# Query-tile constants behind block 6 of a recurrence, and a full-precision sum in the last attention step alone

## The chip, the cores and the metric

One core of a Trainium2 chip. The metric is the device time in microseconds of one execution of the whole program, the median of three runs. Times inside the program come from one profiled execution. Its engines are TensorE (PE, with its weight loads PEld), VectorE (DVE), ScalarE (ACT), GpSimd (POOL) and SyncE (SP, which issues most DMAs); each takes its instructions in the order of its own queue.

## What is computed

One layer of a hybrid trunk on 2064 tokens (16 meta tokens and 2048 of the sequence) of width 1024, all in float32:

```python
p = rms_norm(h, norm_mix_pre) @ w_in
oa = rg_lru_group(...)                  # linear recurrence, 256 columns
ob = forgetting_attention_group(...)    # 8 heads of 64, causal, with a decay
oc = rwkv7_group(...)                   # matrix-state recurrence, 4 heads of 64
h = h + rms_norm(concat(oa, ob, oc) @ w_out, norm_mix_post)
f = causal_dwconv(rms_norm(h, norm_ffn_pre) @ ffn_up, ffn_conv)
h = h + rms_norm((gelu(gate) * val) @ ffn_down, norm_ffn_post)

# attention, per head
s = q @ k.T / 8 + (c[:, None] - c[None, :])      # c: running sum of log f
o = softmax(where(kpos <= qpos, s, -inf)) @ v
# rwkv7, per head and token
S = S * w_t - (S @ kk_t) (kk_t * a_t).T + v_t k_t.T ;  o_t = S @ r_t
```

## The kernel before, in words

Almost all of it keeps full precision by splitting an operand into a rounded part and a remainder and adding three fast products (`mm3`, lines 172 to 176, tiles `psp`, `pswo`, `psu`, `psd`).

The program has four parts. **First** the input projection in three parts of the sequence (lines 2125 and following; tile `psp`). Beside it, generators feed in the two recurrences: `recurrences` runs nine blocks (0 to 8, of 256 tokens, the last of 64). A block of the matrix recurrence has a front (`Rwkv.block`, and `chunks` up to `SOLVED`: scores `rwsc` at lines 1131 and 1136, transposes at 1160, a triangular solve of 15 steps that goes between POOL at 1178 and DVE at 1179) and an ending: small products that complete the inverse (1202 to 1254), **the sums** (lines 1269 to 1271: products `rps`, then `rwgt` and `rwrav` on DVE), **the states** (1281 to 1293: four products one after another, each with a copy to `rstate` at 1293; the fourth copy is the block's last state), and the output with its norm (1320 to 1359). The ending of one block comes after the front of the next, so at the end of the projection the ending of block 5 is under way and the fronts of 7 and 8 and the endings of 6, 7 and 8 are still to come. All these products go through two buffers `rps`, in the order of the program.

**Second** attention (`Attn`). There are 32 steps, of one head and 512 queries each: half 0 with the query blocks 0 and 1, half 1 with 2 and 3. A step has two passes. `maxima` makes rough products (`mx`, line 566) and takes each row's largest (line 571, `mc`), which goes into a row of the query tile `q2` (line 580). `weights` makes exact scores in two products (`sc`, 693 with `q1`, 694 with `q2`), their exp (698, tile `p`), the product with the values (716, `po`) and the sums of the weights (`acc`, 737, on POOL and DVE). The maxima run two steps ahead of the weights, so there are three buffers of each of the query tiles `q3` (for `mx`) and `q2`. Half of the rows of these tiles are constants, set on DVE at the very start of attention, when `Attn` is built: lines 469 and 487 to 489. Attention's first `mx` product needs those of its tiles.

At the end of a step, `ending` queues three pieces of work by a clock of score groups: the column sums of `acc` over partitions, their reciprocals, and the scaling. The sums come in two forms. `total` (767 to 776) splits `acc` on ACT and POOL and adds two fast products (772, 773). `single` (760 to 765) makes one full-precision product (762). The form is chosen by whether the queue for the step's small DMAs is POOL's:

```python
for d, f in zip(self.DELAYS, (single if queue is nc.gpsimd else total, invert, scale)):
```

`run` sets that queue when it comes to the last step. The `ending` of the step before is run inside the last step's `weights`, after its first group of scores, and so takes that queue and `single` too: two steps have it.

**Third** the output projection in 17 tiles (`pswo`), the first of which fill PE between the attention steps of half 1. Tiles 7 and 8 are held until the last but one step has ended; the eviction of tile 9 (line 168) is queued behind the last step's copy of its sums (line 763). **Fourth** the feed-forward layers (`psu`, `psd`).

What sets the order is a scheduler: for each engine it arranges the instructions by a timeline that it works out from their dependencies. `issue_after(x)` adds the rule that an instruction must stand behind `x` in the queue, if both are on the same engine.

Of the kernel before, what the change touches and what calls it, by code (L numbers as in the profile page):

```python
# [8 lines left out]
F32 = mybir.dt.float32  # L9
# [4 lines left out]
ALU = mybir.AluOpType  # L14
# [18 lines left out]
class Core:  # L33


    def __init__(self, tc, ctx):
        self.tc = tc
        self.nc = tc.nc
        self.ctx = ctx
        self.uid = 0  # L40
        nc = self.nc
        self.const = ctx.enter_context(tc.tile_pool(name="const", bufs=1))
        self.ident = self.const.tile([P, P], F32, name="ident")
        make_identity(nc, self.ident[:])
        self.flip = 0
        self.root = self.apart = False
        self.turns = 0

    def n(self, s):
        self.uid += 1  # L50
# [395 lines left out]
class Attn:  # L446
# [7 lines left out]
    def __init__(self, core, pool, psum, more, scr):  # L454
        self.core, self.pool, self.psum, self.more, self.scr = core, pool, psum, more, scr
        self.wide, self.bank, self.place, self.tail = False, 0, 0, False
        nc = self.nc = core.nc
        self.clock, self.later, self.serial, self.added = 0, [], 0, 0
        self.pending, self.loads, self.steps, self.beside = None, [], [], iter(())


        self.turn = {"k": 1, "k2": 1, "q2": 0, "q3": 0}
        self.ring = {s: [] for s in self.turn}
        for i in range(self.AHEAD + 1):
            q3 = pool.tile([P, 512], F32R, tag=f"q3_{i}", name=core.n("q3"), bufs=1)
            self.fixed(q3, None, self.ONES)
            self.ring["q3"].append(q3)
            q2 = pool.tile([P, 512], F32R, tag=f"q2_{i}", name=core.n("q2"), bufs=1)
            nc.vector.memset(q2[64:128].bitcast(F32), 0.0)
            self.ring["q2"].append(q2)  # L470
            if i > 1:
                continue
            k1 = pool.tile([P, 2, KHALF], F32R, tag=f"k1_{i}", name=core.n("k1"), bufs=1)
            self.rear(pool, f"k2_{i}")
            v1 = pool.tile([P, 2, NKT // 2 + 1, 64], F32, tag=f"v1_{i}", name=core.n("v1"), bufs=1)
            self.ring["k"].append((k1, v1))
# [16 lines left out]

    def next(self, s):
        self.turn[s] = (self.turn[s] + 1) % len(self.ring[s])
        return self.ring[s][self.turn[s]]

    def t(self, shape, tag, dt=F32, bufs=2):
# [162 lines left out]
    def weights(self, h, b, keys, queries, fill):  # L661
# [6 lines left out]
        nc, core, scr = self.nc, self.core, self.scr  # L668
        k1, k2, v1 = keys
        q1, q2, bias = queries  # L670
# [71 lines left out]
        def ending(po, acc):  # L742


            while len(self.later) > 8:
                self.later.pop(0)[2]()

            o, oh = self.t([64, 512], "o", bufs=4), self.t([64, 512], "oh")
            c1 = kt[1][2]
            nc.scalar.activation(oh[:, c1:n], po[64:128, c1:n], AF.Copy)  # L750
            if c1:
                nc.scalar.activation(o[:, :c1], po[0:64, :c1], AF.Copy)
            summed = nc.vector.tensor_tensor(o[:, c1:n], po[0:64, c1:n], oh[:, c1:n], op=ALU.add)
            if self.tail:
                self.reduced = summed
            g = n // 16
            dcol = self.t([16, 32], "dcol", bufs=4)
            rb, queue = [], self.queue

            def single():  # L760
                ps = self.mx()
                nc.tensor.matmul(ps[0:1, :n], core.ones_col[:].bitcast(F32), acc[:, :n], start=True, stop=True)
                core.acted = nc.scalar.activation(acc[0:1, :n], ps[0:1, :n], AF.Copy)
                queue.dma_start(scr["den"][h : h + 1, ts], acc[0:1, :n])
                queue.dma_start(dcol[:, :g], scr["den"][h, ts].rearrange("(p c) -> p c", c=g))

            def total():
                ah, al = (self.t([P, 512], "oh", F32R) for _ in range(2))
                core.acted = nc.scalar.activation(ah[:, :n], acc[:, :n], AF.Copy)
                nc.gpsimd.tensor_tensor(al[:, :n], acc[:, :n], ah[:, :n], op=ALU.subtract)  # L770
                ps = self.mx()
                nc.tensor.matmul(ps[0:1, :n], core.ones_col[:], ah[:, :n], start=True, stop=False)
                nc.tensor.matmul(ps[0:1, :n], core.ones_col[:], al[:, :n], start=False, stop=True)
                nc.scalar.activation(acc[0:1, :n], ps[0:1, :n], AF.Copy)
                queue.dma_start(scr["den"][h : h + 1, ts], acc[0:1, :n])
                queue.dma_start(dcol[:, :g], scr["den"][h, ts].rearrange("(p c) -> p c", c=g))

            def invert():
                rb.append(self.t([64, 512], "rb"))
                nc.vector.reciprocal(dcol[:, :g], dcol[:, :g])  # L780
                queue.dma_start(scr["rden"][h, ts].rearrange("(p c) -> p c", c=g), dcol[:, :g])
                queue.dma_start(rb[0][:, :n], scr["rden"][h : h + 1, ts].broadcast_to([64, n]))

            def scale():
                nc.vector.tensor_tensor(o[:, :n], o[:, :n], rb[0][:, :n], op=ALU.mult)
                queue.dma_start(scr["mix"][256 + 64 * h : 256 + 64 * h + 64, ts], o[:, :n])

            for d, f in zip(self.DELAYS, (single if queue is nc.gpsimd else total, invert, scale)):
                self.serial += 1
                self.later.append((self.clock + d, self.serial, f))  # L790
            self.later.sort(key=lambda x: x[:2])
# [31 lines left out]
    def run(self, pool, third):  # L823


        self.queue = self.nc.sync
        ready = []
        for half, bs in enumerate(((0, 1), (2, 3))):
            if half:
                self.rear(third, "k2_2")  # L830
                self.beside = self.meta(pool)
            for h in range(NH):
                self.wide = (half, h) >= WIDE
                keys = self.keys(h, 4 * bs[-1] + 5)
                for b in bs:
                    gen, total, out = self.maxima(h, b, keys), self.pieces(b), []

                    def fill(share, gen=gen, total=total, out=out):
                        while len(out) < min(total, share * total):
                            out.append(next(gen))  # L840

                    if len(ready) == self.AHEAD:
                        self.weights(*ready.pop(0), fill)
                    fill(1.0)
                    ready.append((h, b, keys, next(gen)))
        self.tail = True
        for i, step in enumerate(ready):
            if i == len(ready) - 1:
                self.queue = self.nc.gpsimd
            self.weights(*step, lambda share: None)  # L850
        self.flush()
        for _ in self.beside:
            pass
        while len(self.later) > 1:
            self.later.pop(0)[2]()
# [128 lines left out]
class Rwkv:  # L984
# [127 lines left out]
    def chunks(self, b, nch, sg, rav, bk, wc, bon):  # L1112
# [3 lines left out]
        nc, k, core = self.nc, self.k, self.core  # L1116
        tt = nc.vector.tensor_tensor
# [7 lines left out]
        for c0 in range(0, m2, 4):  # L1125
            m = min(4, m2 - c0)
# [8 lines left out]
            for h, ps in enumerate(pss):  # L1135
                tt(
                    sc[:, 2 * c0 + h : 2 * (c0 + m) : 2, 64:192], ps[:, :m], mask.to_broadcast([P, m, P]),
                    op=ALU.mult,
# [16 lines left out]
        for c in range(0, m2, 4):  # L1155
            m = min(4, m2 - c)
            for src, dst in ((bk, sc), (rav[:, :, 1:3], w3)):
                ps = self.ps().rearrange("p (c t) -> p c t", t=P)
# [48 lines left out]
        for i0, m in groups:  # L1207
            ps = self.ps().rearrange("p (i t) -> p i t", t=32)
# [54 lines left out]
        for c in range(0, m2, 4):  # L1263
            m = min(4, m2 - c)
            ps = self.ps().rearrange("p (c t) -> p c t", t=P)
            for i in range(m):
                for h in range(2):
                    j = 2 * (c + i) + h
                    nc.tensor.matmul(ps[64 * h : 64 * h + 64, i], ap[:, j], sc[0:64, j, 0:128], start=True, stop=True)
            tt(gt[:, c : c + m], ps[:, :m, 0:64], gt[:, c : c + m], op=ALU.add)  # L1270
            tt(rp[:, c : c + m], ps[:, :m, 64:128], rav[:, c : c + m, 0], op=ALU.add)


        st = k["st"]
# [10 lines left out]
        for c in range(nch):  # L1285
            for h in range(2):
                hs = slice(64 * h, 64 * h + 64)
                for p in range(2):
                    nc.tensor.matmul(
                        gain[hs, c, p], gt[hs, p * nch + c], st[hs, c, p], start=False, stop=True,  # L1290
                        skip_group_check=True,
                    )
            nc.vector.tensor_copy(st[:, c + 1], gain[:, c])
        yield

        ntl = -(-nch // 2)
# [1083 lines left out]
```

## Time and profile before

| | us |
|---|---|
| median of 3 runs | 2995.25 (2985.94 to 2998.46) |
| the profiled execution | 2995.96, of it the span 2994.3 |
| last input projection evicted | 878.9 |
| first and last `mx` product of attention | 890.5, 1487.3 |
| full-precision sums of the last two steps | 1508.5, 1540.6 |
| last output-projection product | 1645.2 |
| mean granted clock of TensorE | 0.976 |

The profile is read from the whole to the place: the page's busy shares say which engine has least idle time, the table by stage says where that engine idles and at what clock, and the timelines say what a single instruction waits for. Times are from the start of the span; a clock of 0.50 means that TensorE was granted half of its clock in that stretch.

### The profile page before, as it was taken

The numbers are of one execution on the slowest core, as the hardware profiler recorded it, in microseconds if no ns is written. First come the engines' busy times: TensorE is split into PE (matmuls) and PEld (weight loads), VectorE is DVE, ScalarE is ACT, GpSimd is POOL, SyncE is SP. The second block draws the span as 40 slices with busy tenths as digits, with TensorE's granted clock in tenths as the row PEclk, the third lists the DMA queues.
The fourth block names the chain that finished last, engine by engine and source line by source line (L and its number), as shares of the span: only waits on it lengthen the run. The fifth ranks groups of instructions, "written<-read, shape, count | busy, mean of one in ns | idle before, by whom it ended". The sixth has DMA issues, their size and how long they took to land.

```text
span 2994.3 us, 52802 instructions
## 1 busy us (share of the span) xinstructions
PE 2898.0 (97%) x18694; PEld 2486.3 (83%) x18694; DVE 2037.0 (68%) x3937; ACT 1480.8 (49%) x2858; POOL 1319.7 (44%) x1567
## 2 busy tenths in 40 slices
PE   6999999999999999999999999999999999999998
PEld 6998899888886655665568999999999999787887
DVE  5258644765677776565636998898778787656766
ACT  4246332443346554455634656666565665424333
POOL 1002122121223665666843667446655544656443
PEclk9999899999988999999999999999999999999999
DMA  6777469676644347544336565577777764436453
GB/s 210 239 235 226 135 230 310 203 242 194 199 129 101 95 109 208 134 113 109 77 96 212 183 198 179 173 220 211 208 208 218 222 198 128 158 116 220 145 174 120
DMA packets 469190, 530.49 MB, mean 177 GB/s; under 512 B 85710, under 2 KB 355736, under 8 KB 467372
## 3 DMA queue, kind: packets, MB, share of 16 engines
q1 hardware_dynamic: 468156, 526.17, 58.2%
q8 instruction: 147, 2.41, 0.3%
q0 software_dynamic: 768, 0.93, 0.1%
q14 instruction: 119, 0.97, 0.1%
HBM read 368.07 MB, written 158.90 MB: 176 GB/s over the span
## 4 chain that ended last, share of the span: by engine, by line
PE 59%; DVE 4%; POOL 2%; DMA 2%; ACT 2%; issue 2%; SPq 0%; DVEq 0%; POOLq 0%; ACTq 0%
PE psu L174 9%; PE psu L175 9%; PE psu L176 9%; PE po L716 4%; PE psd L174 4%; PE psd L175 4%; PE psd L176 4%; PE mx L566 2%; PE pswo L174 2%; PE pswo L176 2%; PE pswo L175 2%; PE sc L693 2%; PE sc L694 2%; POOL acc L737 1%; DVE mc L571 1%
## 5 line engine op out<-in xcount | busy, mean ns | idle before, releaser
L175 PE MATMUL psu<-xo,uw 128*128 128x344 f32 x1848 | 591.4, 320 | 0.0
L174 PE MATMUL psu<-xo,uw 128*128 128x344 f32 x1848 | 586.0, 322 | 2.7 <-ACT u L1828 1.2
L176 PE MATMUL psu<-xo,uw 128*128 128x344 f32 x1848 | 581.9, 320 | 1.3 <-POOL uw L1657 1.0
L174 PE MATMUL psp<-xh,wh 128*128 128x384 f32 (+2 forms) x1152 | 380.8, 331 | 0.0
L176 PE MATMUL psp<-xh,wl 128*128 128x384 f32 (+2 forms) x1152 | 378.0, 328 | 0.0
L175 PE MATMUL psp<-xl,wh 128*128 128x384 f32 (+2 forms) x1152 | 377.8, 328 | 0.0
L1657 DVE TENSOR_TENSOR uw<-uq,uw 128x512 fp32r<-128x512 f32 x341 | 320.3, 944 | 59.2 <-ACT uw L1656 56.7
L174 PEld LDWEIGHTS psu<-xo,uw 128*128 128x128 f32 x1848 | 345.8, 188 | 4.3 <-DVE vb L1848 1.8
L176 PEld LDWEIGHTS psu<-xo,uw 128*128 128x128 f32 x1848 | 345.7, 188 | 2.1 <-POOL uw L1657 1.3
L175 PEld LDWEIGHTS psu<-xo,uw 128*128 128x128 f32 x1848 | 347.1, 188 | 0.0
L1656 ACT ACTIVATE uw<-uq 128x512 fp32r<-128x512 f32 x462 | 287.9, 627 | 95.7 <-PE psu L176 44.4
L698 ACT ACTIVATE p<-sc,bias 128x512 f32<-128x512 f32 (+4 forms) x352 | 197.9, 590 | 142.3 <-PE sc L694 119.2
L571 DVE TENSOR_REDUCE mc<-mx 128x1 f32<-128x512 f32 (+6 forms) x352 | 190.0, 565 | 113.6 <-PE mx L566 80.1
L1796 DVE SCALAR_TENSOR_TENSOR uy<-psu,ffn_cols,uy 128x342 f32<-128x342 f32 (+1 forms) x390 | 220.4, 567 | 61.4 <-ACT uy L1794 59.7
L1804 POOL TENSOR_TENSOR uy<-uy,uy 128x342 f32<-128x342 f32 (+1 forms) x132 | 146.5, 1110 | 229.2 <-DVE uy L1796 55.9
L737 POOL TENSOR_TENSOR acc<-acc,p 128x512 f32<-128x512 f32 (+3 forms) x208 | 222.7, 1073 | 48.4 <-DVE acc L737 23.4
L1657 POOL TENSOR_TENSOR uw<-uq,uw 128x512 fp32r<-128x512 f32 x121 | 184.4, 1524 | 133.8 <-ACT uw L1656 116.0
L174 PEld LDWEIGHTS psp<-xh,wh 128*128 128x128 f32 x1152 | 220.1, 191 | 8.7 <-issue 7.3
L176 PEld LDWEIGHTS psp<-xh,wl 128*128 128x128 f32 x1152 | 220.1, 191 | 7.0 <-issue 5.1
L175 PEld LDWEIGHTS psp<-xl,wh 128*128 128x128 f32 x1152 | 220.1, 191 | 5.0 <-issue 3.2
L1657 DVE TENSOR_TENSOR fo<-u,fo 128x896 fp32r<-128x896 f32 x88 | 101.6, 1155 | 133.7 <-ACT fo L1656 133.2
L1656 ACT ACTIVATE fo<-u 128x896 fp32r<-128x896 f32 x88 | 81.2, 923 | 206.6 <-PE psd L176 118.1
(488 smaller groups left out, 6409.4 us busy)
## 6 DMA issues: line engine op xcount, KB each, us to landing
uq<-scr_us SPq DMA_DIRECT2D x220, 256.0 KB
uq<-in_ffn_up_dram SPq DMA_DIRECT2D x209, 256.0 KB
wl<-scr_wk SPq DMA_DIRECT2D x48, 512.0 KB
wh<-scr_wk SPq DMA_DIRECT2D x48, 512.0 KB
u<-scr_ff SPq DMA_DIRECT2D x88, 256.0 KB
scr_ff<-uy SPq DMA_DIRECT2D x110, 171.0 KB
raw<-in_w_in_dram SPq DMA_DIRECT2D x24, 512.0 KB
scr_wk<-wh SPq DMA_DIRECT2D x24, 512.0 KB
```

What stands on the lines that cost most here:

```text
L174: nc.tensor.matmul(out, ah, bh, start=first, stop=False, skip_group_check=more)
L175: nc.tensor.matmul(out, ah, bl, start=False, stop=False, skip_group_check=more)
L176: nc.tensor.matmul(out, al, bh, start=False, stop=last, skip_group_check=more)
L566: nc.tensor.matmul(ps[:rows, : e - a], q3[:, qo : qo + rows], k2[:, a:e], start=True, stop=not last)
L571: self.reduced = nc.vector.tensor_reduce(mc[:rows, i, ci : ci + 1], ps[:rows, : e - a], axis=AX.X, op=ALU.max)
L698: last = nc.scalar.activation(p[:rows, :w], ps[:rows, :w], AF.Exp, bias=bias[:rows, j : j + 1])
L716: mm = nc.tensor.matmul(po[at : at + 64, c0:n], v1[:rows, j], p[:rows, : n - c0], start=start and i < 2, stop=end and i + 2 >= len(group), ...
L737: eng.tensor_tensor(a, ps_[0][0][:rows, c0:n] if start and i == 1 else a, p[:rows, : n - c0], op=ALU.add)
L1656: core.nc.scalar.activation(hi, src, AF.Copy)
L1657: (eng or core.nc.vector).tensor_tensor(lo, src, hi, op=ALU.subtract)
L1796: core.conved = stt(y[:, :n], src[:, i : n + i], cw[:, 44 * i + cc : 44 * i + cc + 1], y[:, :n], op0=ALU.mult, op1=ALU.add)
L1804: core.pooled = nc.gpsimd.tensor_tensor(v[:, :n], g[:, :n], v[:, :n], op=ALU.mult)
```

## The change

Two things. The constants of the query tiles are no longer set when `Attn` is built: each buffer gets them when it is first taken (`next`), and the first buffer's stand behind the sums of the third block from the end, block 6 (`marks[-3]`, `summed`), the other two behind its last state (`moved`). And the sums of the weights are made by `single` only in the `ending` that is run after all steps, which is the last one's; the last but one goes back to `total`, still with POOL's queue for its small DMAs.

```diff
@@ Core.__init__
+        self.marks = []
@@ Attn.__init__
+        self.final = False
...
+        self.blank, self.begun = {s: [] for s in self.turn}, {s: 0 for s in self.turn}
         for i in range(self.AHEAD + 1):
             q3 = pool.tile([P, 512], F32R, tag=f"q3_{i}", name=core.n("q3"), bufs=1)
-            self.fixed(q3, None, self.ONES)
+            self.blank["q3"].append(lambda q3=q3: self.fixed(q3, None, self.ONES))
             self.ring["q3"].append(q3)
             q2 = pool.tile([P, 512], F32R, tag=f"q2_{i}", name=core.n("q2"), bufs=1)
-            nc.vector.memset(q2[64:128].bitcast(F32), 0.0)
+            self.blank["q2"].append(lambda q2=q2: nc.vector.memset(q2[64:128].bitcast(F32), 0.0))
@@ Attn.next
         self.turn[s] = (self.turn[s] + 1) % len(self.ring[s])
+        if self.blank[s] and self.begun[s] < len(self.ring[s]):
+            with self.core.tc.issue_after(self.core.marks[-3][min(self.begun[s], 1)].ins):
+                self.blank[s][self.turn[s]]()
+            self.begun[s] += 1
         return self.ring[s][self.turn[s]]
@@ Attn.weights, ending
-            for d, f in zip(self.DELAYS, (single if queue is nc.gpsimd else total, invert, scale)):
+            for d, f in zip(self.DELAYS, (single if self.final else total, invert, scale)):
@@ Attn.run
+        self.final = True
         self.flush()
@@ Rwkv.chunks
-            tt(rp[:, c : c + m], ps[:, :m, 64:128], rav[:, c : c + m, 0], op=ALU.add)
+            summed = tt(rp[:, c : c + m], ps[:, :m, 64:128], rav[:, c : c + m, 0], op=ALU.add)
...
-            nc.vector.tensor_copy(st[:, c + 1], gain[:, c])
+            moved = nc.vector.tensor_copy(st[:, c + 1], gain[:, c])
+        core.marks.append((summed, moved))
```

With the new code the numbers of later lines grow: 469 becomes 472, lines 487 to 492 become 490 to 495, those from 566 to 857 grow by 7, those from 858 to 1293 by 8, later ones by 9.

The order on DVE at the end of the input projection, before the change: `rwgt_9235` is the ending of block 5, `q_1446` and its neighbours are the query tiles.

```order
L1270 TENSOR_TENSOR rwgt_9235<-rps_9237,rwgt_9235 128x256
L1271 TENSOR_TENSOR rwrav_7292<-rps_9237,rwrav_7292 128x4x64
L487 MEMSET q_1446_11103 64x512
L469 MEMSET q_1447_11107 64x512
L487 MEMSET q_1451_11114 64x512
```

All constants stand between the two halves of block 5's sums and behind them, ahead of and among its states. With the change, DVE where the first constants are now (`rwgt_10203` is the ending of block 6, `rwxu_10567` belongs to block 7):

```order
L1278 TENSOR_TENSOR rwgt_10203<-rps_10216,rwgt_10203 128x256
L1279 TENSOR_TENSOR rwrav_8650<-rps_10216,rwrav_8650 128x4x64
L490 MEMSET q_1451_11110 64x512
L472 MEMSET q_1452_11111 64x512
L491 MEMSET q_1451_11110 3x512
L492 MEMSET q_1451_11110 1x512
L1201 STREAM_TRANSPOSE rwxu_10567<-rwxu_10567 64x512
L1301 COPY rstate<-rps_10228 128x128
```

The first buffer's constants moved back from row 1278 to row 1399 of DVE, past the front of block 7 and the ending of block 6; those of the other two stand 16 rows further on, behind the fourth copy of `rstate`.

PE before the change, just behind the last products of the input projection; `mx` and `sc` are attention's:

```order
L1281 MATMUL rps_9260<-rww_973_7341,rwsc_7340 64x64 x16
L1289 MATMUL rps_9260<-rstate,rwgt_9235 64x64 x4
L1320 MATMUL rps_9298<-rstate,rwrav_7292 64x64
L1289 MATMUL rps_9260<-rstate,rwgt_9235 64x64 x4
L1320 MATMUL rps_9298<-rstate,rwrav_7292 64x64
L566 MATMUL mx_11153<-k_1449_11110,q_1451_11114 128x144
```

And with the change, PE at its first `mx` product:

```order
L1277 MATMUL rps_10205<-rwsc_8670,rwxu_10174 64x128 x8
L1277 MATMUL rps_10216<-rwsc_8670,rwxu_10174 64x128 x8
L1115 MATMUL eps_10501<-rwsq_10443,bones 128x128
L1289 MATMUL rps_10228<-rww_1138_8671,rwsc_8670 64x64 x16
L1297 MATMUL rps_10228<-rstate,rwgt_10203 64x64 x4
L1329 MATMUL rps_10266<-rstate,rwrav_8650 64x64
L573 MATMUL mx_11145<-k_1449_11106,q_1451_11110 128x144
```

Attention's first `mx` product now stands behind the sums of block 6 instead of those of block 5. The 46 rows that it moved past are the rest of block 5's ending, the scores and transposes of block 7, block 6's ending up to its first state, small products of block 8, and two `sc` products of line 700 (693 before), which need no constants.

PE near the end of attention, before the change: `acc_16169` belongs to the last but one step, `sc` to the last.

```order
L694 MATMUL sc_16231<-q_1457_11129,k_1449_11110 128x512
L762 MATMUL mx_16266<-acc_16169,ones_col 1x512
L693 MATMUL sc_16236<-q_2832_15891,k_1453_11120 128x512
L694 MATMUL sc_16236<-q_1457_11129,k_1449_11110 128x512
L716 MATMUL po_16168<-p_16182,v_1455_11124 64x512
```

And with the change, the two products that take its place, among those of output tile 7 (`pswo`):

```order
L176 MATMUL pswo_17080<-wol,mh_17072 128x512
L779 MATMUL mx_16270<-oh_16266,ones_col 1x512
L177 MATMUL pswo_17080<-woh,ml_17073 128x512
L175 MATMUL pswo_17080<-woh,mh_17072 128x512
L176 MATMUL pswo_17080<-wol,mh_17072 128x512
L177 MATMUL pswo_17080<-woh,ml_17073 128x512
L175 MATMUL pswo_17105<-woh,mh_17072 128x512
L176 MATMUL pswo_17105<-wol,mh_17072 128x512
L177 MATMUL pswo_17105<-woh,ml_17073 128x512
L175 MATMUL pswo_17105<-woh,mh_17072 128x512
L780 MATMUL mx_16270<-oh_16267,ones_col 1x512
```

The sums of the last but one step stand some 30 rows later on PE, behind the products with the values and most of output tile 7's first half, and no score of the last step is behind them any more.

## The prediction

> **What bounds the kernel now.** First the page's busy shares and its chain of work that ended last.
>
> ```profile
> span 2994.3 us, 52802 instructions
> PE 2898.0 (97%) x18694; PEld 2486.3 (83%) x18694; DVE 2037.0 (68%) x3937; ACT 1480.8 (49%) x2858; POOL 1319.7 (44%) x1567
> PE 59%; DVE 4%; POOL 2%; DMA 2%; ACT 2%; issue 2%; SPq 0%; DVEq 0%; POOLq 0%; ACTq 0%
> ```
>
> TensorE (PE) is busy for 97% of the span and carries 59% of the chain, so an idle microsecond of PE is lost unless PE idles a microsecond less elsewhere. The change touches the stretch from the last input projection to the last attention step. Next view: busy time by stage (us of the stage; then busy us and instruction count of PE, PEld, DVE, ACT, POOL; then the granted PE clock, the DMA share and GB/s).
>
> ```profile
> 878.00:890.00 12.00, 10.84 (x90) 8.15 (x92) 8.47 (x22) 1.40 (x5) 8.06 (x6) 0.50 0.52 124
> 890.00:974.00 84.00, 77.34 (x693) 56.62 (x695) 64.05 (x188) 47.39 (x104) 28.44 (x53) 0.77 0.48 108
> 974.00:1122.00 148.00, 137.44 (x1207) 88.61 (x1201) 111.90 (x299) 86.49 (x184) 94.30 (x148) 0.94 0.43 103
> 1122.00:1200.00 78.00, 72.16 (x339) 39.59 (x339) 52.41 (x112) 38.26 (x70) 47.11 (x53) 0.93 0.73 207
> ```
>
> From 890 to 1122 PE is kept 92 to 93% busy because two things run side by side: the tail of the recurrence (blocks 5 to 8), a long chain of small products and DVE operations, and the first attention steps. The rows that fix the places:
>
> ```profile
> 878.88 0.42 DVE L241 SCALAR_TENSOR_TENSOR stl<-psp,sth 128x256 fp32r<-128x256 f32 x1 [0.66 <-ACT sth L240]
> 882.95 0.48 DVE L487 MEMSET q<- 64x512 f32 x1 [0.16 <-issue]
> 887.31 0.41 DVE L1271 TENSOR_TENSOR rwrav<-rps,rwrav 128x256 f32<-128x256 f32 x1
> L566 PE MATMUL mx<-k,q x352: 219/397/797, 890.5 to 1487.3; 128*128 128x512 f32 x72, 128*128 128x400 f32 x51, 128*128 128x128 f32 x16, 128*128 128x384 f32 x16
> 886.58 3.60 POOL L492 MEMSET k<- 1x2080 f32 x2
> L1271 DVE TENSOR_TENSOR rwrav<-rps,rwrav x2: 414/414/414, 970.9 to 973.2; 128x256 f32<-128x256 f32 x2
> ```
>
> The last projection is evicted at 878.9. The query constants are set from 882.95, the sums of block 5 end at 887.7, the first product of attention starts at 890.5, and the sums of block 6 end at 973.6.
>
> **The change, part by part: the constants.** By the order of the changed kernel the first constants stand behind the sums of block 6, and the first mx product behind them, with 46 rows of recurrence on PE that no attention product can pass (but for two sc products). The instructions are the same; what moves is all attention work that now lies between 890 and 974. So the sum is: the new start of attention, plus that work, less 974.
>
> *New start.* From the sums of block 5 (887.7) to those of block 6 (973.6) the chain takes 85.9 us with attention beside it. I cut it in four stages, at these ends:
>
> ```profile
> 917.01 0.42 DVE L1357 TENSOR_TENSOR rww<-rww,rps 128x256 f32<-128x256 f32 x1
> 925.77 0.69 DVE L1136 TENSOR_TENSOR rwsc<-rps,rmask 128x512 f32<-128x512 f32 x1 [0.23 <-PE rps L1131]
> 940.01 0.67 DVE L1212 TENSOR_TENSOR rwxu<-rps,rmask 64x512 f32<-64x512 f32 x1
> ```
>
> Whether PE runs at full or half clock there decides much, so clock rows first, four microseconds each: projections, then recurrence alone, then mostly attention.
>
> ```profile
> 872.00:876.00 4.00, 4.00 (x29) 3.19 (x28) 1.90 (x5) 1.04 (x4) 0.00 (x0) 1.00 0.20 68
> 880.00:884.00 4.00, 4.00 (x22) 2.17 (x20) 2.14 (x5) 1.02 (x4) 3.52 (x3) 0.50 0.86 218
> 884.00:888.00 4.00, 4.00 (x52) 3.55 (x54) 3.40 (x10) 0.00 (x0) 2.53 (x3) 0.50 0.42 98
> 916.00:920.00 4.00, 4.00 (x25) 2.42 (x23) 2.70 (x7) 2.77 (x7) 3.78 (x4) 1.00 0.77 176
> ```
>
> With the recurrence alone the clock stands at 0.50, though PE counts as busy for all 4 us. The Trainium skill (TensorE: Matmul & The Clock Gate, section on the HAM clock gate) says that the clock is full after about 3.4 us of sustained PE activity and half after an idle window of that length. Taken literally it would put the new stretch, in which PE has products most of the time, at full clock (the low ends below, about 9 us under the value taken); the trace does not agree, with 0.50 from 880 to 888 at 4.00 of 4.00 busy, and the measurement decides.
>
> The stages, now without attention:
>
> ```profile
> 887.70:917.40 29.70, 9.01 (x19) 0.55 0.86 184
> 918.15 1.16 PE L1131 MATMUL rps<-rwrav,rwbk 64*128 64x128 f32 x8
> 921.21 0.70 PE L1440 MATMUL eps<-rwlu,lru_ga_w 128*128 128x256 f32 x2
> 934.00 1.28 ACT L698 ACT_TABLE_LOAD   x1
> 940.70:973.60 32.90, 5.31 (x160) 4.96 (x160) 0.79 0.19 45
> 940.70:973.60 32.90, 3.93 (x32) 3.56 (x32) 0.79 0.19 45
> 940.70:973.60 32.90, 5.22 (x32) 4.09 (x32) 0.79 0.19 45
> 940.70:973.60 32.90, 2.18 (x32) 1.70 (x32) 0.79 0.19 45
> ```
>
> - Stage 1 (state, output of block 5; 29.7 us): attention's DVE reductions in it are 9.0 us (first row), the query constants some 2.5 more; the raw-row loads and the dependent small DVE operations stay. I let a little over half of that go: 23.2.
> - Stage 2 (scores of block 7; 9.1 us): four groups of 1.16 us and two gate pairs of about 1.2 us are 7.0 us at full clock, some 13 at half clock. So 7 to 13.
> - Stage 3 (transposes, first small products; 14.2 us): what goes is attention's exp and the table load it needs, about 3 us: 11.3.
> - Stage 4 (rest of block 6; 32.9 us): the last four rows are PE's time by line (L1202, L1244, L1254, L1269), 16.6 us at a mean clock of 0.79, so 13.2 at full clock; half clock makes at most twice that, and as part is latency I take 24. With about 5 us of evictions between them: 18 to 29.
>
> Together 59.5 to 76.5 us, so block 6's sums at 947 to 964; four memsets of 0.5 us follow, and attention starts at 949 to 966. I take **958**, the middle: rows show the half clock for recurrence alone, but parts of the chain are DVE's.
>
> *Work moved.* How much attention was done before 974, and what is it worth? Reductions (L571), then scores (L694), in three windows:
>
> ```profile
> 890.00:974.00 84.00, 18.34 (x38) 0.77 0.48 108
> 1122.00:1200.00 78.00, 35.96 (x65) 0.93 0.73 207
> 1400.00:1508.00 108.00, 39.76 (x70) 1.00 0.32 77
> 890.00:974.00 84.00, 10.15 (x27) 5.73 (x27) 0.77 0.48 108
> 1122.00:1200.00 78.00, 16.65 (x45) 8.65 (x45) 0.93 0.73 207
> 1400.00:1508.00 108.00, 32.77 (x91) 16.57 (x91) 1.00 0.32 77
> ```
>
> In the two windows without recurrence and without output projection attention does 110 pieces in 78 us and 161 in 108, 1.41 to 1.49 a microsecond. The 65 pieces before 974 are then worth 44 to 46 us; but they are the narrow ones (18.34/38 = 0.48 us a reduction against 0.55), so I take **39**. If some slip into PE's idle time of the two stages behind (148 - 137.4 and 78 - 72.2, 16 us), it is 29. Ends: 29 to 46.
>
> At 958 the recurrence stands where it stood at 974, so the loss is 958 + 39 - 974 = **+23 us** (+4 to +38).
>
> **The other part: one full-precision product in the last step alone.** Now the last but one step has it too:
>
> ```profile
> 1505.94 0.40 PE L694 MATMUL sc<-q,k 128*128 128x512 f32 x1
> 1508.52 1.87 PE L762 MATMUL mx<-acc,ones_col 128*1 128x512 f32 x2 [2.18 <-DVE acc L737]
> 1497.28 1.27 POOL L770 TENSOR_TENSOR oh<-acc,oh 128x512 fp32r<-128x512 f32 x1
> 1525.26 0.55 POOL L786 DMA_DIRECT2D scr_mix<-o  x1 [1.33 <-DVE o L785]
> 1541.65 0.59 ACT L763 ACTIVATE acc<-mx 1x512 f32<-1x512 f32 x1 [2.46 <-PE mx L762]
> 1542.14 1.04 ACT L168 ACTIVATE mh<-raw 128x1024 fp32r<-128x1024 f32 x1
> ```
>
> PE idles 2.18 us before this product and spends 1.87 on it. In the changed order the scores go on, and the sums are two short products behind output-projection work (about 0.23 us each): 2.18 + 1.87 - 0.46 = **3.6 us** gained. The price is a copy on ACT and a subtraction of 1.27 us on POOL (L770), and the result some 5 us later. What waits for it is the load of output tile 9, whose eviction (L168 at 1542.1) is queued behind the last step's own copy (L763 at 1541.7), while the result was stored at 1525.3: about 14 us of cover. Without that cover the 3.6 would become a loss of about 1.5; POOL idles for several microseconds there, so the addition is hidden. Ends: -4 to 0.
>
> **Sum.** 23 - 3.6 = +19 us on the profiled execution's own 2996.0 (span 2994.3 and 1.7 around it), 3015; the median shown, 2995.25, is 0.7 below. I forecast **3014 us**, +0.6%. A measurement of this kernel can tell about 0.5%, 15 us, from no change.
>
> **The rivals.**
> - *The tail is better done alone* (ends faster). Mechanism: in the long stretch PE has steady small products and its clock goes to 1.00, so attention starts at 949; the rest of the recurrence, no longer strewn through as many steps, lets PE idle less up to 1200. Price: 949 + 29 - 974 = +4, - 3.6 for the other part, and half of the 31 us of idle time and lost clock in the two stages (10.6 + 148 x 0.06 + 5.8 + 78 x 0.07) back: -15, **2981**. It decides if attention starts before about 943, or if half of those 31 us go. For it: PE's 93% hides lost clock. Against: the 0.50 in the rows of recurrence alone, and that the freed time is already counted in the 29. That is also where the skill's clock rule would lead.
> - *Later start, slow restart.* The chain gains almost nothing because DVE waits in order behind block 7's solve, and attention restarts at half clock, as it did in the trace (0.50 in the row of 884, 1.00 only in that of 916): start 966, 46 of work, 8 of restart (an estimate: a third of the 26 us from 890 to 916), the other part worth nothing: 966 + 46 + 8 - 974 = +46, **3042**. For it: DVE's order interleaves the solve with the chain. Against: stage 1 loses 9 us of attention's reductions in any case.
> - *The constants do not hold anything* (the change doesn't do what it says): attention waits for its keys on POOL and SP, not for the constants, and only 3.6 us remain: **2992**. For it: POOL's constants of the keys (L492) end only at 890.2, just ahead of the first product. Against: they stand on POOL where they stood, ahead of the whole new stretch.
>
> **How the numbers follow.** Forecast 70%, spread over 3000 to 3030; tail alone 10%; slow restart 15%; no hold 5%. The range 2992 to 3035 takes the forecast with its ends and most of the slow restart. Faster by over 0.5% (below 2980): 8%, within: 34%, slower (above 3010): 58%.
>
> **What would show it.** In the changed profile: the first L573 product (the new line of mx) near 958 and not 890; the clock near 0.5 from 880 to there; PE's busy share clearly under 90% from 890 to 958; block 6's sums (L1279) 10 to 26 us earlier than 973; no product of L769 (new line of the full-precision sums) before the last step; attention's last product some 19 us later than 1541, and everything behind shifted by as much. I am wrong if the start is before 945, if the end of attention moves by under 8 us, or if the time behind attention changes by more than 5 us.

## The result, and the profile after the change

| | before | changed |
|---|---|---|
| median of five runs, us | 2995.25 (2985.94 to 2998.46) | 3048.01 (3033.79 to 3053.23) |
| ratio | | 1.0171, 95% interval 1.0152 to 1.0190 |
| span of the profiled execution, us | 2994.3 | 3046.3 |

The changed kernel is **slower by 53 us**, 1.7%. The forecast was 3014 us in a range of 2992 to 3035: the sign was right, the size was not.

First the places that the prediction named, in the changed kernel: the last sums of block 6 (the second row of L1279), the constants behind them, and the groups of attention's first products, of the full-precision sums and of the first products of the feed-forward layers.

```profile
952.42 0.41 DVE L1279 TENSOR_TENSOR rwrav<-rps,rwrav 128x256 f32<-128x256 f32 x1
954.13 0.41 DVE L1279 TENSOR_TENSOR rwrav<-rps,rwrav 128x256 f32<-128x256 f32 x1
954.71 0.48 DVE L490 MEMSET q<- 64x512 f32 x1 [0.16 <-issue]
L573 PE MATMUL mx<-k,q x352: 220/397/895, 957.0 to 1541.7; 128*128 128x512 f32 x74, 128*128 128x400 f32 x51, 128*128 128x384 f32 x17, 128*128 128x256 f32 x13
L769 PE MATMUL mx<-acc,ones_col x2: 590/612/634, 1590.7 to 1591.1; 128*1 128x512 f32 x2
L175 PE MATMUL psu<-xo,uw x1848: 315/321/488, 1697.6 to 2589.8; 128*128 128x344 f32 x185
```

Attention starts at 957.0, where the forecast had 958. But its last `mx` product is 54.4 us later (1541.7 against 1487.3), and the first product of the feed-forward layers 51.7 us (1697.6 against 1645.9, a row below); from there to the end of the span both kernels take 1348 us. So all of the loss arises between 890 and about 1590. The table by stage of the changed kernel, in the windows that the prediction showed of before:

```profile
878.00:890.00 12.00, 11.19 (x109) 8.35 (x111) 3.34 (x11) 1.02 (x4) 8.23 (x6) 0.50 0.56 130
890.00:974.00 84.00, 66.19 (x626) 54.38 (x621) 56.60 (x168) 31.18 (x69) 11.26 (x27) 0.54 0.34 73
974.00:1122.00 148.00, 134.88 (x1045) 88.56 (x1044) 97.34 (x274) 76.99 (x163) 75.91 (x120) 0.84 0.35 87
1122.00:1200.00 78.00, 65.75 (x322) 36.15 (x320) 42.64 (x103) 39.28 (x79) 45.84 (x71) 0.91 0.51 118
```

In every one of the last three windows PE is less busy than before (66.2 for 77.3, 134.9 for 137.4, 65.8 for 72.2 us) and runs at a lower granted clock (0.54 for 0.77, 0.84 for 0.94, 0.91 for 0.93). The first of these was forecast. That the next two lose as well, though the recurrence is ahead there, was not.

To see where the time went I cut at the new start of attention and take PE's busy time alone (then its instructions, clock, DMA share, GB/s). Of the kernel before:

```profile
890.00:957.00 67.00, 60.34 (x553) 0.75 0.59 130
957.00:1008.00 51.00, 48.22 (x380) 0.95 0.36 88
1008.00:1122.00 114.00, 106.22 (x965) 0.93 0.40 98
1200.00:1500.00 300.00, 297.38 (x1352) 1.00 0.45 107
890.00:1645.90 755.90, 724.39 (x4213) 0.95 0.48 126
```

and of the changed one:

```profile
890.00:957.00 67.00, 52.82 (x512) 0.53 0.42 89
957.00:1008.00 51.00, 44.95 (x422) 0.73 0.20 51
1008.00:1122.00 114.00, 103.31 (x742) 0.85 0.38 92
1200.00:1500.00 300.00, 290.54 (x1324) 0.98 0.52 136
890.00:1697.60 807.60, 750.83 (x4194) 0.91 0.45 118
```

The last row of each runs up to the first feed-forward product. It splits the 51.7 us in two: PE idles 807.6 - 750.8 = 56.8 us where it idled 31.5 (+25.3), and it is busy 26.4 us longer with the same products, at a lower clock.

The other rows say when. Busy time times granted clock is roughly PE's work in microseconds at full clock (roughly, since the clock is a mean over the window). Up to 957: 45.3 before, 28.0 now, 17.3 lost. From 957 to 1008: 45.8 and 32.8, 13.0 lost. To 1122: 98.8 and 87.8, 11.0 lost. To 1200 (rows of the tables by stage): 67.1 and 59.8, 7.3 lost. **So up to 1200, 17 us are lost while attention waits, and another 31 after it has started.** From 1200 on PE was busy for 297.4 of 300 us at a clock of 1.00 before, so there is next to no room to make up what is missing by then. The changed kernel falls a little short there too (290.5 us at 0.98, 12.7 us less work), which makes 60 us of missing work by 1500 for a shift of 51.7. The count is good to some ten microseconds, not better.

### The profile page after: what moved, and what is told of

It is laid out like the page before. It is cut to its first block, busy times and chain, and to the rows that moved or that the text cites. A ratio compares the mean times of both kernels' runs of the same rounds, so it can differ in the third digit from the quotient of the medians.

```text
span 3046.3 us, 52803 instructions
## 1 busy us (share of the span) xinstructions
PE 2928.7 (96%) x18694; PEld 2511.4 (82%) x18694; DVE 2037.0 (67%) x3937; ACT 1483.0 (49%) x2859; POOL 1322.1 (43%) x1568
## 4 chain that ended last, share of the span: by engine, by line
PE 59%; DVE 4%; DMA 3%; POOL 2%; issue 1%; ACT 1%; SPq 1%; DVEq 0%; POOLq 0%; ACTq 0%
PE psu L175 9%; PE psu L176 9%; PE psu L177 9%; PE psd L175 4%; PE psd L176 4%; PE psd L177 4%; PE po L723 4%; PE pswo L175 2%; PE pswo L177 2%; PE pswo L176 2%; PE mx L573 2%; PE sc L700 2%; PE sc L701 1%; DVE mc L578 1%; DMA scr_den<-acc 1%
```

## The experiments

A difference in microseconds is against the kernel before, by medians of the runs made beside it. Theory A was that the whole loss is the late start; B that the other part of the change costs most of it; C that the loss is in how the scheduler lays out everything behind, not in the delay.

**One part at a time.** First the sums alone, on the kernel before, then the constants alone, on the changed kernel:

```diff
+        self.final = False
...
-            for d, f in zip(self.DELAYS, (single if queue is nc.gpsimd else total, invert, scale)):
+            for d, f in zip(self.DELAYS, (single if self.final else total, invert, scale)):
...
+        self.final = True
```

> Only the second part of the change: the kernel before, with the full-precision sum in the very last step alone; the constants stay where they were. Theory A (the whole loss comes from attention's late start, and my price of -4 to 0 us for this part holds): 2991 to 2996 us. Rival B (my +23 us for the late start was right, and giving the last-but-one step the two fast products costs the rest, because the column sums now stand behind ACT, POOL and the output projection): about 3020 to 3030 us, the loss of this part alone some 30 us.

Measured: 2992.07 us against 2993.30, ratio 0.9994 (0.9982 to 1.0006). The part is worth -1 us, between -5 and +2. B falls.

> Only the first part of the change: the constants behind block 6 as in the changed kernel, the full-precision sums in the last two steps as before. Theory A: as slow as the changed kernel or up to 4 us slower, 3048 to 3053 us. Rival B: 3015 to 3020 us.

Its edit, on the changed kernel, puts the condition of the first diff back. Measured: 3052.35 us, ratio 1.0197 (1.0179 to 1.0214), +59. The constants alone carry the whole loss. Attention starts at 950.6 here, 6 us earlier than in the changed kernel, and the kernel is no faster for it.

**Where the constants stand.** One number sets the block behind whose sums and last state they stand:

```diff
-            with self.core.tc.issue_after(self.core.marks[-3][min(self.begun[s], 1)].ins):
+            with self.core.tc.issue_after(self.core.marks[-4][min(self.begun[s], 1)].ins):
```

> The changed kernel with one number changed: the constants stand behind the sums and the last state of block 5 (the fourth block from the end), where they came to stand by themselves in the kernel before. Theory A: attention starts near 890 again and nearly all the loss is gone, 2988 to 2998 us. Rival C (it isn't the late start: setting each buffer's constants at its first use, apart from each other, or the new order that the scheduler makes of what follows, costs the time): still over 3025 us.

Measured: 2997.91 us, ratio 1.0015 (1.0000 to 1.0030), +5. With the constants still set at their first use, but behind block 5, attention starts at 881.8 and nearly all of the loss is gone. So setting them buffer by buffer does not cost it, and a new order need not: by their traces, a third of DVE's operations between 850 and 1520 stand in another order here than in the kernel before. C as it was stated falls. But a later start always comes with an order of its own, and no run here holds the one fixed and moves the other.

A point between the two, `masked` being the operation that masks the scores of block 7's front:

```diff
-            with self.core.tc.issue_after(self.core.marks[-3][min(self.begun[s], 1)].ins):
+            with self.core.tc.issue_after(self.core.scores7.ins):
...
-                tt(
+                masked = tt(
...
+        if b == 7:
+            core.scores7 = masked
```

> The changed kernel with the constants of all three buffers behind the masked scores of block 7's front, a point that lies between block 5's last state (nearly no loss) and block 6's sums (+53 to +59 us). Run alone, the recurrence passes it near 925 (915 to 930), 30 to 40 us behind the start before. Theory A (each us by which attention starts later costs 0.8 us, as 53/66.5 between those two points): +25 to +32, 3018 to 3026 us. Rival T (the loss comes from the ending of block 6 being done alone and in one piece, with its small products at half clock, not from the delay before it): at most +12, under 3006 us.

Measured: 3021.18 us, ratio 1.0088 (1.0062 to 1.0115), +25, as theory A said; rival T falls. Up to here the loss grows with the delay of the start, 0.8 to 0.9 us for each us.

Then later than the change, with `marks[-2]` and `marks[-1]`:

> The changed kernel with the constants behind block 7 (the second from the end), so that attention starts later still. Theory A: the recurrence alone reaches block 7's sums about 60 us behind block 6's, near 1015, and ends near 1060; attention then has some 160 pieces (maxima and scores) fewer than the kernel before had at 1104, at the 0.8 us a piece that the changed kernel took for its missing ones behind 1081; 131 - 44 = +87 us on the kernel before, about 3083 us (3070 to 3100). Theory A', my prediction's rate (0.6 us a piece, since the narrow ones come first): about 3050 us. Rival C (the cost is the rearrangement, not the delay): within 15 us of the changed kernel, 3033 to 3063 us, which A' can be told from by attention's progress.

Measured: 3060.74 us, ratio 1.0226 (1.0206 to 1.0247), +67. Attention starts 51 us later than in the changed kernel and only 15 us more are lost. That is outside the range of A, and above A' as well; the 0.8 doesn't hold beyond block 6. It lies in the band that I gave C, whose first half the run behind block 5 rules out. So I formed another theory, from PE's work:

> The changed kernel with the constants behind the last block, block 8: the recurrence and attention one after the other. Busy time of PE between 890 and 1200 times its granted clock was 255.4 us before, 231.0 with the constants behind block 7's scores (+25 us), 208.1 in the changed kernel (+53), 199.0 behind block 7 (+67). Theory E (what is lost is PE's work in this stretch, whoever does it, since from 1200 on PE is 97 to 99% busy and gives nothing back): the recurrence alone does 46.9 us of such work in the 118 us up to 1008, 0.40 a microsecond, and attention alone some 0.82; 30 us more of the one for the other cost 13 us, so +80, about 3075 us (3066 to 3084). Theory A (0.8 us for each microsecond of later start): start near 1040, +120, over 3100 us. Rival R (a recurrence that is done earlier gives its PE time to attention): attention alone is no slower than beside the recurrence, and the whole stays where it was with block 7, 3055 to 3063 us.

Measured: 3067.91 us, ratio 1.0243 (1.0224 to 1.0261), +74, inside the range of theory E and outside those of A and R. PE's row from 890 to 1200 in seven kernels: the kernel before; constants behind block 7's scores; the changed kernel; behind block 7; behind block 8; then behind block 5, and the constants alone behind block 6.

```profile
890.00:1200.00 310.00, 286.94 (x2229) 0.89 0.52 131
```

```profile
890.00:1200.00 310.00, 275.02 (x2054) 0.84 0.47 116
```

```profile
890.00:1200.00 310.00, 266.82 (x1990) 0.78 0.39 91
```

```profile
890.00:1200.00 310.00, 255.19 (x1907) 0.78 0.38 88
```

```profile
890.00:1200.00 310.00, 249.23 (x1879) 0.72 0.37 83
```

```profile
890.00:1200.00 310.00, 278.57 (x2157) 0.91 0.50 128
```

```profile
890.00:1200.00 310.00, 263.89 (x1952) 0.79 0.39 91
```

| constants behind | first `mx` | last state of the recurrence | PE's work to 1200 (busy x clock) | missing | measured |
|---|---|---|---|---|---|
| where they were (before) | 890.5 | 1104.5 | 255.4 | | |
| block 5 | 881.8 | 1082.9 | 253.5 | 1.9 | +5 |
| block 7's scores | 917.6 | 1056.3 | 231.0 | 24.4 | +25 |
| block 6 (the change) | 957.0 | 1081.4 | 208.1 | 47.3 | +53 |
| block 6, constants alone | 950.6 | 1075.1 | 208.5 | 46.9 | +59 |
| block 7 | 1007.9 | 1051.6 | 199.0 | 56.4 | +67 |
| block 8 | 1043.9 | 1040.7 | 179.4 | 76.0 | +74 |

The reader is to see two things. The measured loss follows the missing work (within 12 us) and not the start. And an early end of the recurrence does not make up for it: behind block 7's scores it is done 48 us earlier than before, and the kernel is 25 us slower; behind block 5 it is done 22 us earlier, and the kernel is no faster.

**Is the low clock a cause?** Dense products that nobody reads go ahead of the recurrence's own, first in all its buffers from the end of the projection on, in the changed kernel and in the one before:

```diff
+    warm = 0
...
-        return self.psum.tile([P, 512], F32, tag="at", name=self.core.n("rps"), bufs=2)
+        ps = self.psum.tile([P, 512], F32, tag="at", name=self.core.n("rps"), bufs=2)
+        for i in range(self.warm):
+            idb = self.core.identb
+            self.nc.tensor.matmul(ps[:, P * i : P * i + P], idb[:], idb[:], start=True, stop=True)
+        return ps
...
+        R.warm = 4
         beside.finish()
```

> The changed kernel with extra work: from the end of the input projection on, each buffer that the matrix recurrence takes for its products first gets four dense 128x128 products in bfloat16 that nobody reads (439 in all). By the two profiles PE's loss between 890 us and the first product of the feed-forward layers is 25 us of idle time and 26 us of longer products at a lower granted clock (0.78 against 0.89 up to 1200). Theory K: the low clock while the recurrence runs alone is what makes the lone stretch long and half of the loss; dense products raise it, block 6's sums come before 945 and the whole is under 3038 us, although the dummies cost PE time. Rival L: the lone stretch is a chain of dependent steps, the clock of TensorE only stretches products that something else would wait for anyway; the dummies cost 0.05 to 0.1 us each, block 6's sums come at 957 or later, and the whole is 3055 to 3090 us.

Measured: 3046.34 us, ratio 1.0162 (1.0134 to 1.0190), the clock from 890 to 957 still 0.53. Neither theory had this: the whole is too slow for K and too fast for L. Attention starts at 967.7 here, 11 us later than in the changed kernel, and the whole is no slower: once more the time does not follow the start.

> As the run with four dense products, with one in each buffer (110 in all). Theory K: if one is enough for the clock, under 3040 us; if not, 3048 to 3056. Rival L: 3048 to 3058 us, with the granted clock as in the changed kernel.

Measured: 3047.69 us, ratio 1.0179 (1.0158 to 1.0200), within a microsecond of the lower end that both gave; with the clock at 0.50 it tells nothing of K.

> The kernel before with four dense 128x128 bfloat16 products ahead of each use of the recurrence's buffers from the end of the projection on. In the changed kernel these 439 products added 9 us of busy time and left the whole where it was (3046 against 3048 us), the granted clock between 957 and 1200 rising from about 0.85 to 0.90. Theory K: in the kernel before too the clock rises from 0.89 in the stretch from 890 to 1200, and PE, 93% busy there, gains: under 2985 us. Rival L: PE has no room for them; 2998 to 3015 us.

Measured: 3012.66 us, ratio 1.0058 (1.0042 to 1.0075), +19: where PE has no room the extra products cost time, and the clock from 890 to 1200 stayed at 0.89. This is L.

Then more of them, and only between block 5's and block 6's last state:

```diff
+        for _ in range(12 if len(self.core.marks) == 6 else 0):
+            self.nc.tensor.matmul(
+                ps[:, 0:256], self.core.identb[:], self.core.ident[:].bitcast(BF16), start=True, stop=True
+            )
```

> The changed kernel with far more extra work on PE, and only up to block 6's sums: each buffer taken for the recurrence's products between block 5's and block 6's last state gets twelve dense 128x256 products in bfloat16 first that nobody reads (some 430). With four 128x128 ones the granted clock between 890 and 957 stayed at 0.53 and PE's busy time at 52.6 of 67 us, so they were too few to say what holds the clock. Theory K (the clock follows how much PE has to do): it is over 0.85 up to block 6's sums, the recurrence's own products take half as long there, and although the dummies need some 46 us of PE themselves, the sums come before 975 and the whole is under 3062 us. Rival L (the clock in this stretch does not follow PE's load): it stays near 0.5, the dummies take some 90 us at half clock, the sums come after 1000 and the whole is over 3070 us.

Measured: 3043.86 us, ratio 1.0161 (1.0144 to 1.0179); the clock rose to 0.90, attention started at 963.1. The clock does follow what PE does, as K said.

> As the run with twelve dense products in each of the recurrence's buffers between block 5's and block 6's last state, but with four. Twelve raised the granted clock of 890 to 957 from 0.53 to 0.90, yet took 36 us of PE there themselves, and attention started at 963 instead of 957. Four take a third, some 12 us, about PE's idle time there (14 us). Theory K (the low clock is what makes the lone stretch long): if four are enough for a clock over 0.8, attention starts before 952 and the whole is under 3038 us. Rival L (the stretch is a chain of waits between engines, which a faster PE hardly shortens): even with the clock over 0.8 attention starts at 952 to 960 and the whole is 3040 to 3050 us. If the clock stays under 0.65, the run does not tell them apart.

> The same with seven dense products in each buffer, some 21 us of PE in the lone stretch, in case four are too few for the clock. Theory K: clock over 0.8, attention starts before 956, the whole under 3040 us. Rival L: clock over 0.8, attention starts at 956 to 964, the whole 3040 to 3050 us.

Measured: 3057.42 us with four, ratio 1.0204 (1.0188 to 1.0221), start at 966.0; 3060.40 us with seven, ratio 1.0213 (1.0196 to 1.0230), start at 970.8. Neither theory had them so slow. PE in the lone stretch with none (the row of the changed kernel above: 52.82 us busy at 0.53), four, seven and twelve:

```profile
890.00:957.00 67.00, 55.89 (x514) 0.68 0.40 84
```

```profile
890.00:957.00 67.00, 59.18 (x514) 0.67 0.37 75
```

```profile
890.00:957.00 67.00, 59.26 (x646) 0.90 0.33 67
```

Four and seven cost 9 and 12 us against the changed kernel; twelve, with the most to do and the highest clock, cost none and are 16.5 us faster than seven. More work in less time is what a clock that matters looks like, but it isn't shown: the dummies also change the order of everything else. Aligned with the changed kernel's, between 850 and 1520, some 90 of DVE's 1000 operations stand elsewhere with four, 160 with twelve and 210 with seven. And no run had the full clock without its price in PE time, so how much of the 53 us a full clock alone would give back stays open. None of these kernels beat the one before.

## Why the prediction was wrong, point by point

- **The change does what its words say, and attention's new start: right.** Forecast 958 (949 to 966), measured 957.0. Block 6's sums end at 954.5 instead of 973.6, 19 us earlier, within the 10 to 26. The clock is 0.50 from 878 to 890 and 0.53 to 957, PE is busy for 52.8 of 67 us (79%). That it came out within a microsecond is in part luck. Block 5's sums end at 885.3, 2.4 us before the 887.7 that the stages were counted from, and the four stages took 20.4, 11.2, 9.4 and 28.2 us, where the prediction had 23.2, 7 to 13, 11.3 and 18 to 29: the first and the third came out 2 to 3 us shorter, the last near its upper end, and the misses cancel.
- **The work moved, W = 39 us: this is the step that failed.** With the measured end the sum "958 + 39 - 974" reads 957 + W - 974 = 51.7, so W was 69. What was wrong is the rate by which the 65 pieces were priced. 1.41 to 1.49 pieces a microsecond were read in windows of the kernel before in which attention has PE to itself and keeps it 93 to 97% busy, and were used for a restart beside blocks 7 and 8 of the recurrence. Reductions, then scores, of the changed kernel, and below them the kernel before:

```profile
890.00:974.00 84.00, 3.70 (x9) 0.54 0.34 73
974.00:1081.00 107.00, 25.79 (x53) 0.81 0.31 79
1122.00:1200.00 78.00, 29.66 (x56) 0.91 0.51 118
890.00:974.00 84.00, 2.07 (x5) 0.54 0.34 73
974.00:1081.00 107.00, 16.05 (x45) 0.81 0.31 79
1122.00:1200.00 78.00, 14.87 (x44) 0.91 0.51 118
```

```profile
974.00:1081.00 107.00, 25.05 (x53) 0.94 0.38 93
974.00:1081.00 107.00, 17.27 (x53) 0.94 0.38 93
```

  From its start at 957 to 1081, where the recurrence now ends, attention does 14 + 98 = 112 pieces, 0.90 a microsecond. The kernel before did 65 + 106 = 171 from 890.5 to 1081, also 0.90: that was the rate beside the recurrence. With it the 65 pieces cost 72 us, and the prediction's own sum gives 957 + 72 - 974 = +55. With the constants behind block 8, where attention is alone from its start, it does 218 pieces from 1043.9 to 1200, 1.40 a microsecond: the rate that was taken holds for attention alone. (From 1122 to 1200, alone as well but at other steps, the changed kernel does 56 + 44 = 100 pieces where the kernel before did 110.)
- **"At 958 the recurrence stands where it stood at 974"**: the sum credits this lead of 16 us in full. The sum alone can't tell a smaller lead from a larger W, but attention's progress shows how little it made up: 67 pieces are done by 1040, as many as the kernel before had soon after 974; at 1081 it is 59 pieces behind, at 1200 some 70, and its last `mx` product is 54.4 us late. Of the 66.5 us by which it starts later it makes up 12, where the forecast counted on some 44 (67.5 us later for a loss of 23). In PE's work, the prediction counted about the first 17 us that are missing and not the 31 behind the start. The 29 that it allowed for work "slipping into idle time" went the wrong way: there is more idle time, not less.

  Why PE does less behind the start is shown in part. From 957 on it runs at a lower clock than before (0.73 for 0.95 up to 1008). From 1122 to 1200 the recurrence has no more than 0.4 us on PE in either kernel, and PE idles for 12.3 us where it idled 5.8. Most of the difference is attention waiting for its own exp (first the changed kernel, then the one before):

```profile
PE sc L700 <- ACT p L705: 8.6, 6, 4.6
```

```profile
PE sc L693 <- ACT p L698: 1.7, 5, 0.5
```

  The longest of these waits is a chain: the scores wait for the exp, the exp for POOL's sums of the weights, and these for the DMA that stores the column sums of an earlier step.

```profile
1192.64 1.26 POOL L744 TENSOR_TENSOR acc<-p,p 128x512 f32<-128x512 f32 x1 [5.21 <-DMA scr_den<-acc]
1193.93 1.26 ACT L705 ACTIVATE p<-sc,bias 128x512 f32<-128x512 f32 x2 [7.91 <-POOL acc L744]
1194.67 0.79 PE L700 MATMUL sc<-q,k 128*128 128x512 f32 x1 [4.56 <-ACT p L705]
```

  The kernel before did the same share of attention (pieces 158 to 257) in the 81 us from about 1071 to 1152, with 10.5 us of the recurrence's products on PE in between; the changed kernel, alone, takes 78. So here the PE time that the recurrence left free was hardly used. That its products had filled these gaps fits this, but no run tests it by itself.
- **The full-precision sums, -3.6 us (-4 to 0): in its range, but not shown to be more than nothing.** The run with this part alone gave -1 (-5 to +2). The price of the two short products, 0.23 us each, was right: their rows say 0.39 and 0.40, but products overlap, and the next one starts 0.23 us behind.

```profile
1568.58 0.39 PE L779 MATMUL mx<-oh,ones_col 128*1 128x512 f32 x1
1568.81 0.39 PE L177 MATMUL pswo<-woh,ml 128*128 128x512 f32 x1
1570.66 0.40 PE L780 MATMUL mx<-oh,ones_col 128*1 128x512 f32 x1
1590.66 1.06 PE L769 MATMUL mx<-acc,ones_col 128*1 128x512 f32 x2 [2.08 <-DVE acc L744]
```

  The wait of about 2 us ahead of the last full-precision product stays: it is there in the last step too. What became of the 2.18 us that the last but one step should save, no run shows apart from the noise.
- **Time behind attention: right.** 1348.4 us before and 1348.7 now from the first feed-forward product to the end of the span.
- **The rivals.** "Later start, slow restart" gave 3042, close in number, through a start at 966 that did not come; the restart was real, but work and restart, 46 + 8 = 54 us there, were 69. (Its 3042 also lies above the range's end of 3035, so the range did not take "most of the slow restart", as the prediction says.) "The tail is better done alone" fell with the clock rows, and with the run behind block 7's scores, where an earlier end of the recurrence went with a slower kernel. "The constants hold nothing" fell with the start at 957.

## What to carry to other kernels

In this kernel, when one of two overlapping streams was moved later, the price was not the moved work at the rate that it reaches when it is alone. What followed the measured times to some ten microseconds was how much the bounding engine gets done, busy time times clock, until the next stretch in which it is saturated, in both arrangements. A stream that finishes earlier is a gain only if what remains can use the engine by itself; read that from a window in which it is alone. And read the rate of a restart in a window where the other stream still runs.

## What was not expected of the hardware

PE can count as busy for a long stretch and still stand at half clock. With the constants behind block 7's scores:

```profile
926.00:956.00 30.00, 30.00 (x213) 0.50 0.08 18
```

Thirty of 30 us, at 0.50, mostly with products of 32 and 64 rows and some of attention's 128-row products between them. Twelve dense products in each buffer raised the clock of the stretch from 890 to 957 from 0.53 to 0.90 with PE busy for 59.3 of 67 us; four and seven reached 0.68 and 0.67. The Trainium skill (TensorE: Matmul & The Clock Gate, section on the HAM clock gate) ties the clock to TensorE's recent activity; the twelve agree with that, the 30 us do not if busy time in the profile is taken for activity. What the monitor counts, no run here shows.
